# A two-layer recurrent decoder step on one core: small-tile work cut from VectorE, norm roots and first remainders moved off GpSimd, the planner's costs re-read from the trace

## The chip, the cores and the metric

One core of a Trainium2 chip runs the whole program. The metric is the device time of one execution in microseconds (us); the kernel before takes 1069.55 us, the median of three runs (1068.46 to 1069.59). About 0.2% of it, 2.1 us, is what a measurement of this kernel can tell from no change.

## What is computed

One inference step of a decoder with two layers, on 1024 prompt tokens and 8 x 4 sample tokens (1056 columns in all, model width 1024). Layer 0 is an RG-LRU block, layer 1 an HGRN2 block:

```
xn = rmsnorm(x) * g_norm                        # mean of squares over 1024 features, rsqrt, gain
u  = xn @ w_in;  xb, gate = u[:1536], u[1536:]  # layer 0: 1024 -> 3072
xc = causal_conv(xb, conv_w, conv_b)            # 4 taps
r, ig = sigmoid(xc @ w_r + b_r), sigmoid(xc @ w_i + b_i)   # 16 blocks of 96
log_a = -8 * softplus(-lam) * r;  a = exp(log_a)
h_t = a_t * h_(t-1) + sqrt(1 - a_t^2) * (ig * xc)_t        # a scan over time
x  = x + (h * silu(gate)) @ w_out
...                                             # layer 1: HGRN2, 1024 -> 4096, matrix states, 1024 -> 1024
y  = rmsnorm(x) * final_gain
```

The conv states, the hidden states and the matrix states are outputs too. Everything is float32. A product is made of three passes on TensorE: each operand is parted into a rounded "high" part and the "remainder" (value minus high), and high x high, high x remainder and remainder x high are added up in PSUM. So each weight tile and each activation tile costs a cast on ScalarE (high) and a subtraction on VectorE or GpSimd (remainder) before TensorE can use it.

## The kernel before

**Tiling.** Features lie on the 128 partitions, tokens on the free axis, in three chunks of 352 columns (`c` = 0, 1, 2). A weight is a block of 128 x 1024, loaded as two raw tiles of 128 x 512. `weights()` loads it, casts the high part on ScalarE (L388) and subtracts the remainder on the engine it is told (L333, in `subtract`).

**The start of layer 0** (`begin`, from L862). Six weight blocks (three of the gate, three of the conv branch, `items`) and the three chunks of x are loaded. For chunk 0 the high and remainder parts are made of x times the gain without waiting for the norm, which is applied to the products later (L490, L537). In parallel `squares` (L432 on) adds up the squares of the eight feature tiles of each chunk: the square on ScalarE (L440) or, for the pairs that the list `MU` names, on GpSimd (L438), the running sum on VectorE (L443). `norm` (L445) then makes the factor: a TensorE product with ones adds over the partitions (L286), two VectorE operations scale and add the epsilon (L455), GpSimd raises to the power -0.5 (L457), VectorE spreads the factors over two diagonals (L458, L461), and TensorE broadcasts them (L463). `scaled_parts` (L465) multiplies x by gain and factor on VectorE (L468), casts the high part on ScalarE (L469) and subtracts the remainder (L333) on VectorE, or on GpSimd for every fourth feature tile. `VI` names the weight blocks whose remainders VectorE makes: 0, 1, 2 and 4; those of 3 and 5 are GpSimd's.

Then come the 18 products of the six blocks with the three chunks, the convolution (L506 to L515), the gates of the recurrence (`lru`, L549: Tanh at L573 and L579, Exp at L586, Tanh at L588, Sqrt at L596, the scan at L613), and so on through layer 0. `norm` is called three times here and three times more near the end of layer 0 (`out_last`, L658), where layer 1's input is normed.

**Small tiles.** `smalls` (L748) works out per-feature constants from the parameters on tiles of 128 x 12: half the two gate biases (`hbr`, `hbi`), a rearranged copy of them for the 32-partition rows (`hbd`), and 8 * softplus in a form with one Exp and a polynomial of eight steps, as `cn` and `cp`. It issues 34 VectorE operations (recorded at L750) and one Exp on ScalarE (L761). Each `norm` adds a VectorE memset of its factor tile (L450), six in all. All operations of `smalls` write one key, `sm`, for which the Tanh of L573 and L579 wait, as do L586 and L588. `smalls1` (L782, recorded at L783) and `masks` (L804, recorded at L808) make constants of layer 1 in the same way; `masks` uses two of the five `k` buffers, which the norms and the recurrence use too.

**What sets the order.** No queue order is written by hand. Each operation is handed to a planner (`Flow.add`, L68) with its engine, a cost in us, what it reads and writes and a priority. `plan` simulates the engines on the host with these costs; `run` plans forward, then backward for due times, eight times over, and keeps the best; `search` tries 3000 variations of the first 60 us. The instructions are then issued in that order, a fixed queue for each engine. The costs: `HOP` is what a result takes to reach another engine; between two operations of the same engine `lag` is nothing. A VectorE operation costs 0.075 or 0.13 us and 0.00104 us for each column, a GpSimd operation 0.13 and 0.0022. Operations that are flagged `both` and GpSimd operations delay one another in the plan as if they shared a port. Small-tile operations (`seq`, L744) are planned at 0.1 us, without that flag. Layer 0 and layer 1 are planned one after the other by the same class.

Of the kernel before, what the change touches and what calls it, by code (L numbers as in the profile page):

```python
# [51 lines left out]
class Flow:  # L52

    HOP = {"PE": 0.22, "DVE": 0.14, "ACT": 0.14, "POOL": 0.14, "SP": 0.2}
    ENGINES = ("PE", "DVE", "ACT", "POOL", "SP")
    TURNS = 8
    ends = []
# [13 lines left out]
    def add(self, eng, us, emit, r=(), w=(), prio=5, kb=0, main=False, both=False):  # L73


        i = len(self.ops)
        deps = set()
        for k in r:
            if k in self.writer:
                deps.add(self.writer[k])  # L80
        for k in w:
            if k in self.writer:
                deps.add(self.writer[k])
            deps.update(self.readers.get(k, ()))
        if main:
            if self.main is not None:
                deps.add(self.main)
            self.main = i
        for k in w:
            self.writer[k] = i  # L90
            self.readers[k] = []
        for k in r:
            self.readers.setdefault(k, []).append(i)
        deps.discard(i)
        self.ops.append((eng, us, emit, deps, prio, kb, self.side if eng == "PE" and not main else 0.0, both))

    def lag(self, i, j):

        a, b = self.ops[i], self.ops[j]
        if a[0] == b[0] and not a[5]:  # L100
            return 0.0
        return self.HOP[a[0]] + b[6] + (2.15 + a[5] / 250.0 if a[5] else 0.0)

    def plan(self, key, stop=None):

        n = len(self.ops)
        left = [len(o[3]) for o in self.ops]
        ready = [0.0] * n
        wait = {e: [] for e in self.ENGINES}
        free = dict(self.busy)  # L110
        dma = locked = taken = 0.0
        for i in range(n):
            if not left[i]:
                wait[self.ops[i][0]].append(i)
        starts, ends, took, order = [0.0] * n, [0.0] * n, [0.0] * n, []
        for _ in range(n):
            t0, e = min((max(free[e], min(ready[i] for i in q)), e) for e, q in wait.items() if q)
            q = wait[e]
            i = min((j for j in q if ready[j] <= t0), key=lambda j: (key[j], j))
            q.remove(i)  # L120
            order.append(i)
            _, us, _, _, _, kb, _, both = self.ops[i]
# [95 lines left out]
def tile_trunk(ctx: ExitStack, tc: tile.TileContext, xT, prm, hc, w0, wg, wo0, w1, wo1, s_in,  # L218
# [22 lines left out]
    def pv(name):  # L241
        return P[:, PRM[name][0]:PRM[name][1]]
# [62 lines left out]
    with ExitStack() as l0:  # L305
# [20 lines left out]
            fl.add("DVE", own + 0.00104 * n, emit, r, w, prio, both=both)  # L326

        def pool(n, emit, r, w, prio=5):
            fl.add("POOL", 0.13 + 0.0022 * n, emit, r, w, prio)

        def subtract(e, n, b, x, a, r, w, prio):

# [15 lines left out]
            cycle([(wts.tile([128, 512], dt, tag=tag, bufs=n, name="w" + tag), (tag, i)) for i in range(n)])  # L348
            for tag, n, dt in (("raw", NRAW, F32), ("hi", NW, F32R), ("lo", NW, F32R)))
        nrs = cycle([(fixed(f"nr{i}", [128, 4]), ("nr", i)) for i in range(2)])  # L350
        xbs = ring("xb", 3, 384)
        ks = [(KR[:, chunk(i)], ("k", i)) for i in range(KB)]
        ts, xrs = cycle(ks[:3]), cycle(ks[3:])
# [88 lines left out]
                e = eng or G  # L442
                (pool if e is G else dve)(CH, lambda: e.tensor_tensor(a[:, :CH], a[:, :CH], sq, op=ALU.add), (sk, ak), (ak,), 2)  # L443

        def norm(acc, own=None):  # L445

            a, ak = acc
            r, rk = next(nrs)
            dg, dk = own or next(xbs)
            dve(4, lambda: V.memset(r, 1.0), (), (rk,), 0)  # L450
            f = CH // 128
            ps, pk = next(hg)
            fl.add("PE", 0.7, lambda: norm_sum([ps[:, i:i + 1] for i in range(4)], a, CH, True, True), (ak,), (pk,), 0)
            for q, src in ((slice(0, f), ps[:, :f]), (slice(f, f + 1), ps[:CH % 128, f:f + 1])):
                dve(4, lambda q=q, src=src: V.tensor_scalar(r[:src.shape[0], q], src, 1.0 / D, EPS, op0=ALU.mult, op1=ALU.add),  # L455
                    (pk,), (rk,), 0)
            fl.add("POOL", 0.9, lambda: G.tensor_tensor(r[:, :3], r[:, :3], mhalf[:, :3], op=ALU.pow), (rk,), (rk,), 0)  # L457
# [89 lines left out]
        def lru(g):  # L547
# [11 lines left out]
            for c in range(NCH):  # L559
# [5 lines left out]
                for i, hb in ((0, hbr), (1, hbi)):  # L565
                    for j in range(3):
                        m = 3 * g + j
                        ps, pk = next(hg)
                        (a, ak), (b, bk) = xpart(j, 0, c), xpart(j, 1, c)
                        u = 3 * i + j  # L570
                        fl.add("PE", 0.48, lambda ps=ps, a=a, b=b, u=u: mm3(ps[:, :CH], (gh[:, u, :], gl[:, u, :]), a, b, True, True),
                               (ak, bk, ("gh", u // 4 * 4), ("gl", u // 4 * 4)), (pk,), 0)
                        act(CH, lambda ps=ps, R=R, i=i, j=j, hb=hb, m=m: S.activation(R[:, i, j], ps[:, :CH], AF.Tanh, bias=hb[:, m:m + 1],  # L573
                                                                           scale=0.5), (pk, ("sm",)), (("R", s, i, j),), 2, 0.1)
                    ps, pk = next(hg)

                    fl.add("PE", 0.62, lambda ps=ps, i=i, c=c: T.matmul(ps[:96, :CH], gs[:, i, :], ST[:96, chunk(c)], start=True, stop=True),  # L577
                           (("gs",), *(("ST", j, c) for j in range(3))), (pk,), 0)
                    act(CH, lambda ps=ps, i=i: S.activation(td[:, i], ps[:96, :CH], AF.Tanh, bias=hbd[:96, 4 * i + g:4 * i + g + 1],  # L579
                                                            scale=0.5), (pk, ("sm",)), (("td", i),), 2, 0.1)  # L580
# [162 lines left out]
        def seq(keys, prio, *emits):  # L743

            for eng, emit in emits:
                fl.add(eng, 0.1, emit, (("P",),), keys, prio)

        def smalls():  # L748
            def v(f, *a, **k):
# [2 lines left out]
            def ttv(o, a, b, op):  # L752
                v(V.tensor_tensor, o, a, b, op=op)

            nonlocal hbr, hbi, hbd, cn, cp
            hbr, hbi, nl, t1, e, z, z2, po = (small(12) for _ in range(8))
            v(V.tensor_scalar, hbr, pv("br"), 0.5, None, op0=ALU.mult)
            v(V.tensor_scalar, hbi, pv("bi"), 0.5, None, op0=ALU.mult)
            v(V.tensor_scalar, nl, pv("lam"), -1.0, None, op0=ALU.mult)
            ttv(t1, pv("lam"), nl, ALU.min)  # L760
            seq((("sm",),), 0.5, ("ACT", lambda: S.activation(e, t1, AF.Exp)))  # L761
            v(V.tensor_scalar, t1, e, 2.0, None, op0=ALU.add)
            v(V.reciprocal, z, t1)
            ttv(z, z, e, ALU.mult)
            ttv(z2, z, z, ALU.mult)
            v(V.tensor_scalar, po, z2, 1.0 / 17, 1.0 / 15, op0=ALU.mult, op1=ALU.add)
            for d in (13, 11, 9, 7, 5, 3, 1):
                ttv(po, po, z2, ALU.mult)
                v(V.tensor_scalar, po, po, 1.0 / d, None, op0=ALU.add)
            ttv(po, po, z, ALU.mult)  # L770
            v(V.tensor_scalar, nl, nl, 0.0, None, op0=ALU.max)
            cp, cn = small(12), small(12)
            v(V.scalar_tensor_tensor, cp, po, 2.0, nl, op0=ALU.mult, op1=ALU.add)
            v(V.tensor_scalar, cn, cp, -4.0, None, op0=ALU.mult)
            v(V.tensor_scalar, cp, cp, 2.0, None, op0=ALU.mult)
            hbd = small(8)
            for i, hb in ((0, hbr), (1, hbi)):
                for j in range(3):
                    w = slice(32 * j, 32 * j + 32)
                    v(V.tensor_copy, hbd[w, 4 * i:4 * i + 4], hb[w].rearrange("p (g j) -> p g j", j=3)[:, :, j])  # L780
# [73 lines left out]
        g0s = [g0[:, k:k + 1] for k in range(KD)]  # L854
        bcs = free[11]
        accs = next(xbs), free[9], free[10]
        VI, XG, MU = (0, 1, 2, 4), (), [(0, k) for k in range(1, 8, 2)]
        rest = [(o[:, a:a + 512], ("a", i, a)) for i, o in enumerate(a_rows) for a in (0, 512)]
        rest += [(ST[:, :512], *(("ST", j, c) for j in range(3) for c in range(2)))]
        raw1 = [(), rest[:1], rest[1:3], rest[3:5], (), ()]  # L860
# [1 line left out]
        def begin(c, first, last):  # L862
# [20 lines left out]
                act(CH, lambda bc=bc: S.copy(bcs[0], bc), (bk,), (bcs[1],), 0)  # L883
            else:
                for k, (x, xk) in enumerate(raw[c]):
                    scaled_parts(c, k, x, xk, bc, bk, g0s[k], ("g0",), G if k % 4 == 3 else V)

        def products(c):
            for i in (2, 0, 1, 3, 4, 5) if c else range(6):
# [935 lines left out]
```

## Time and profile before

| | us |
|---|---|
| median of three runs | 1069.55 (1068.46 to 1069.59) |
| the profiled execution, its own time | 1070.2 |
| its span, first to last instruction | 1068.4 |
| busy: TensorE | 1042.6 (98%) |
| busy: VectorE | 809.9 (76%) |
| busy: ScalarE | 576.0 (54%) |
| busy: GpSimd | 498.9 (47%) |

How to read it: PE is TensorE, DVE VectorE, ACT ScalarE, POOL GpSimd, SP the engine that issues most DMAs. `L333` is line 333 of the kernel. A group or a row of the timeline shows start, duration, engine, line and tiles (`out<-in`). The chain of work that ended last is followed back from the last instruction: each of its pieces shows when it began, how long it held the chain, and the engine and line. "issue" is time for which the profile shows no wait. A table by stage shows for each stretch of the span its length, then the busy time of each engine with the number of its instructions, the granted TensorE clock (1.00 is full), the share of the DMA engines and GB/s.

### The profile page before, as it was taken

To read this page: it belongs to the slowest core of one execution; us is meant where nothing else is said; L and a number is where in the kernel's file an instruction comes from. 1 tells how busy PE (TensorE), PEld (TensorE's weight loads), DVE (VectorE), ACT (ScalarE), POOL (GpSimd) and SP (SyncE) were. 2 spreads that over 40 slices of the span, in tenths; PEclk is the share of its full clock that TensorE was granted. 3 is DMA by queue.
4 is the path that set the end of the run, shared out by engine and by line. 5 is a ranking of instruction groups with operands and counts; after the bars stand their busy time and mean duration, and the time that the engine had idled before them with its cause. 6 is when DMAs were issued, how large, how long until landed. Compare 5 with 4: busy or idle time off the path is not lost.

```text
span 1068.4 us, 26448 instructions
## 1 busy us (share of the span) xinstructions
PE 1042.6 (98%) x10244; PEld 1010.2 (95%) x10244; DVE 809.9 (76%) x1620; ACT 576.0 (54%) x1311; POOL 498.9 (47%) x587
## 2 busy tenths in 40 slices
PE   9898999999999999999999999999999999999997
PEld 8788999999999999999989999999999999999986
DVE  8998767589698789544487989797969796985536
ACT  5476645966856686434354463636454554552324
POOL 2425233445344355744524555555555555642544
PEclk9999999999999999999999999999999999999998
DMA  8201112212581388553374233332324242576204
GB/s 293 67 14 56 33 48 61 67 44 66 180 271 52 95 247 263 153 170 129 99 228 138 73 123 106 106 118 85 135 74 140 83 140 83 168 232 204 85 1 163
DMA packets 92013, 130.72 MB, mean 122 GB/s; under 512 B 11632, under 2 KB 70000, under 8 KB 91888
## 3 DMA queue, kind: packets, MB, share of 16 engines
q1 hardware_dynamic: 89584, 126.28, 37.1%
q10 hardware_dynamic: 2304, 2.77, 0.7%
q8 instruction: 80, 1.31, 0.5%
q14 instruction: 45, 0.37, 0.1%
HBM read 85.93 MB, written 38.20 MB: 116 GB/s over the span
## 4 chain that ended last, share of the span: by engine, by line
PE 86%; DVE 9%; issue 2%; DMA 1%; POOL 1%; ACT 0%; SPq 0%; POOLq 0%; DVEq 0%; ACTq 0%
PE mm L249 24%; PE mm L251 24%; PE mm L250 24%; PE hg L1066 2%; PE hg L1274 1%; PE hg L577 1%; PE hg L1276 1%; PE hg L250 1%; PE hg L251 1%; PE hg L249 1%; DVE xl L333 1%; DVE sg L468 1%; DVE R L443 1%; DVE k L509 1%; DVE smalls L750 1%
## 5 line engine op out<-in xcount | busy, mean ns | idle before, releaser
L249 PE MATMUL mm<-xh,whi 128*128 128x352 f32 (+1 forms) x1127 | 352.8, 313 | 0.0
L251 PE MATMUL mm<-xh,wlo 128*128 128x352 f32 (+1 forms) x1127 | 348.8, 310 | 0.0
L250 PE MATMUL mm<-xl,whi 128*128 128x352 f32 (+1 forms) x1127 | 348.4, 309 | 0.0
L333 POOL TENSOR_TENSOR wlo<-wraw,whi 128x256 fp32r<-128x256 f32 (+3 forms) x188 | 199.3, 1075 | 248.6 <-ACT whi L388 135.4
L250 PEld LDWEIGHTS mm<-xl,whi 128*128 128x128 f32 x1127 | 213.3, 189 | 1.5
L249 PEld LDWEIGHTS mm<-xh,whi 128*128 128x128 f32 x1127 | 212.9, 189 | 1.7
L251 PEld LDWEIGHTS mm<-xh,wlo 128*128 128x128 f32 x1127 | 213.0, 189 | 0.0
L509 DVE SCALAR_TENSOR_TENSOR k<-xb,prm_sb,k 128x352 f32<-128x352 f32 (+2 forms) x144 | 87.0, 615 | 23.1 <-ACT k L506 20.0
L249 PE MATMUL mm<-t,whi 128*128 128x264 f32 (+1 forms) x330 | 96.6, 293 | 1.4 <-DVE attns L1073 1.4
L250 PE MATMUL mm<-t,whi 128*128 128x264 f32 (+1 forms) x330 | 94.6, 287 | 0.0
L251 PE MATMUL mm<-t,wlo 128*128 128x264 f32 (+1 forms) x330 | 94.4, 286 | 0.0
L1504 DVE TENSOR_TENSOR k<-mm,k 128x264 f32<-128x264 f32 x154 | 64.4, 425 | 21.6 <-PE mm L251 20.2
L333 POOL TENSOR_TENSOR wlo<-R,whi 128x256 fp32r<-128x256 f32 x70 | 59.7, 873 | 29.7 <-ACT whi L1431 26.2
L592 POOL TENSOR_TENSOR k<-X 128x352 f32<-128x352 f32 x36 | 44.2, 1234 | 47.2 <-DVE R L593 32.8
L249 PEld LDWEIGHTS mm<-t,whi 128*128 128x128 f32 x330 | 62.1, 188 | 2.2 <-ACT krep L1006 1.6
L251 PEld LDWEIGHTS mm<-t,wlo 128*128 128x128 f32 x330 | 62.2, 189 | 0.0
L250 PEld LDWEIGHTS mm<-t,whi 128*128 128x128 f32 x330 | 62.2, 188 | 0.0
L1431 ACT CAST whi<-wraw 128x512 fp32r<-128x512 f32 x56 | 34.6, 617 | 45.8 <-PE mm L251 15.4
L388 ACT CAST whi<-wraw 128x512 fp32r<-128x512 f32 (+2 forms) x79 | 43.9, 572 | 24.9 <-PE mm L250 20.2
L249 PE MATMUL mm<-yh,whi 128*128 128x352 f32 x153 | 51.4, 336 | 0.0
L251 PE MATMUL mm<-yh,wlo 128*128 128x352 f32 x153 | 49.4, 323 | 0.0
L250 PE MATMUL mm<-yl,whi 128*128 128x352 f32 x153 | 49.4, 323 | 0.0
(460 smaller groups left out, 2520.0 us busy)
## 6 DMA issues: line engine op xcount, KB each, us to landing
wraw<-in_w_dram SPq DMA_DIRECT2D x88, 256.0 KB, 2.8
wraw<-in_wo_dram SPq DMA_DIRECT2D x34, 192.0 KB, 2.5
R<-in_w_dram SPq DMA_DIRECT2D x17, 256.0 KB, 2.7
si<-in_s_in_dram SPq DMA_DIRECT2D x8, 512.0 KB, 4.8
vt<-sg SPq DMA_DIRECT2D x8, 512.0 KB, 3.2
kt<-kt SPq DMA_DIRECT2D x8, 512.0 KB, 2.7
sg<-vt SPq DMA_DIRECT2D x32, 128.0 KB, 2.9
kt<-kt SPq DMA_DIRECT2D x32, 128.0 KB, 3.5
```

The costliest lines, as they stand in the source:

```text
L249: T.matmul(out, wh, xh, start=first, stop=False)
L250: T.matmul(out, wh, xl, start=False, stop=False)
L251: T.matmul(out, wl, xh, start=False, stop=last)
L333: emit = lambda: e.tensor_tensor(b, x, a.bitcast(F32), op=ALU.subtract)
L388: act(m, lambda hi=hi, raw=raw, m=m: S.copy(hi[:, :m], raw[:, :m]), rk, (hk,), prio)
L443: (pool if e is G else dve)(CH, lambda: e.tensor_tensor(a[:, :CH], a[:, :CH], sq, op=ALU.add), (sk, ak), (ak,), 2)
L468: dve(CH, lambda: V.scalar_tensor_tensor(x, x, g, bc, op0=ALU.mult, op1=ALU.mult), (xk, bk, gk), (xk,), prio)
L509: dve(u, lambda src=src, dst=dst, sh=sh, k=k: V.scalar_tensor_tensor(dst, sh(src, k), pc("cw", 12 * k + m), dst, op0=ALU.mult, op1=ALU.add ...
L592: pool(CH, lambda x=x, a=a, b=b: G.tensor_tensor(x, a.bitcast(F32), b.bitcast(F32), op=ALU.add), (ak, bk), (xk,), 3)
L1066: T.matmul(ps[32 * j:32 * j + 32, n * w:n * w + w], B[:, o:o + 32], q(slice(o, o + 32)), start=True, stop=True, tile_position=(0, 32 * j))
L1431: act(512, lambda: S.copy(hi, raw), (rk,), (hk,), 2)
L1504: dve(QT, lambda: V.tensor_tensor(o[0], z[0], u[0], op=ALU.add), (z[1], u[1]), (o[1],), 0)
```

## The change

It has four parts. (1) `smalls`: biases are halved and rearranged on ScalarE (one multiplication for both, three copies), under a key of their own, `smb`, for which alone L573 and L579 wait; the polynomial's steps are one fused operation each; `cn` and `cp` are made on ScalarE. (2) `norm`: the factor tile is set to one once, at the start; ScalarE takes Sqrt of sum / 1024 + epsilon, straight from PSUM, once for each 128 columns (three times), and VectorE takes one reciprocal. (3) `VI` takes in all six blocks, `MU` is empty, and the remainders of chunks 1 and 2 in `begin` (L886) are all VectorE's; those of chunk 0 (L898) and of `out_last` (L714) stay as they were, every fourth on GpSimd. (4) The planner: a result costs its own engine 0.1 us on VectorE and ScalarE (`SAME`), a GpSimd operation 0.15 instead of 0.13, a small-tile operation 0.09 instead of 0.1, and those of VectorE carry the flag `both`. The order is planned anew with these costs, for both layers.

```diff
+    SAME = {"DVE": 0.1, "ACT": 0.1}
...
         if a[0] == b[0] and not a[5]:
-            return 0.0
+            return self.SAME.get(a[0], 0.0) if i in b[8] else 0.0
...
-            fl.add("POOL", 0.13 + 0.0022 * n, emit, r, w, prio)
+            fl.add("POOL", 0.15 + 0.0022 * n, emit, r, w, prio)
...
         nrs = cycle([(fixed(f"nr{i}", [128, 4]), ("nr", i)) for i in range(2)])
+        for r, _ in islice(nrs, 2):
+            V.memset(r, 1.0)
...
-            dve(4, lambda: V.memset(r, 1.0), (), (rk,), 0)
-            f = CH // 128
-            ps, pk = next(hg)
-            fl.add("PE", 0.7, lambda: norm_sum([ps[:, i:i + 1] for i in range(4)], a, CH, True, True), (ak,), (pk,), 0)
-            for q, src in ((slice(0, f), ps[:, :f]), (slice(f, f + 1), ps[:CH % 128, f:f + 1])):
-                dve(4, lambda q=q, src=src: V.tensor_scalar(r[:src.shape[0], q], src, 1.0 / D, EPS, op0=ALU.mult, op1=ALU.add),
-                    (pk,), (rk,), 0)
-            fl.add("POOL", 0.9, lambda: G.tensor_tensor(r[:, :3], r[:, :3], mhalf[:, :3], op=ALU.pow), (rk,), (rk,), 0)
+            if sums is None:
+                ps, pk = next(hg)
+                sums, sumk = [ps[:, i:i + 1] for i in range(4)], [pk]
+                fl.add("PE", 0.7, lambda: norm_sum(sums, a, CH, True, True), (ak,), sumk, 0)
+            for i, (s, (_, u)) in enumerate(zip(sums, spans(CH))):
+                act(4, lambda i=i, s=s, u=u: S.activation(r[:u, i:i + 1], s[:u], AF.Sqrt, bias=epsc[:u], scale=1.0 / D), sumk, (rk,), 0,
+                    0.1 if i else 0.8)
+            dve(4, lambda: V.reciprocal(r[:, :3], r[:, :3]), (rk,), (rk,), 0, True)
...
-                                                                           scale=0.5), (pk, ("sm",)), (("R", s, i, j),), 2, 0.1)
+                                                                           scale=0.5), (pk, ("smb",)), (("R", s, i, j),), 2, 0.1)
...
-                fl.add(eng, 0.1, emit, (("P",),), keys, prio)
+                fl.add(eng, 0.09, emit, (("P",),), keys, prio, both=eng == "DVE")
...
-            hbr, hbi, nl, t1, e, z, z2, po = (small(12) for _ in range(8))
-            v(V.tensor_scalar, hbr, pv("br"), 0.5, None, op0=ALU.mult)
-            v(V.tensor_scalar, hbi, pv("bi"), 0.5, None, op0=ALU.mult)
-            v(V.tensor_scalar, nl, pv("lam"), -1.0, None, op0=ALU.mult)
-            ttv(t1, pv("lam"), nl, ALU.min)
-            seq((("sm",),), 0.5, ("ACT", lambda: S.activation(e, t1, AF.Exp)))
+            hb, nl, t1, e, z, z2, po, cp, cn = small(24), *(small(12) for _ in range(8))
+            hbd, hbr, hbi = small(8), hb[:, :12], hb[:, 12:]
+            other(lambda: S.mul(hb, P[:, PRM["br"][0]:PRM["bi"][1]], 0.5), "smb")
+            for j in range(3):
+                w = slice(32 * j, 32 * j + 32)
+                other(lambda w=w, j=j: S.copy(hbd[w].rearrange("p (i g) -> p i g", i=2), hb[w].rearrange("p (i g j) -> p i g j", i=2, j=3)[:, :, :, j]), "smb")
+            v(V.scalar_tensor_tensor, t1, pv("lam"), -1.0, pv("lam"), op0=ALU.mult, op1=ALU.min)
+            other(lambda: S.activation(e, t1, AF.Exp))
+            v(V.tensor_scalar, nl, pv("lam"), -1.0, 0.0, op0=ALU.mult, op1=ALU.max)
...
-            for d in (13, 11, 9, 7, 5, 3, 1):
-                ttv(po, po, z2, ALU.mult)
-                v(V.tensor_scalar, po, po, 1.0 / d, None, op0=ALU.add)
-            ttv(po, po, z, ALU.mult)
-            v(V.tensor_scalar, nl, nl, 0.0, None, op0=ALU.max)
...
+            ttv(po, po, z2, ALU.mult)
+            for d in (13, 11, 9, 7, 5, 3):
+                v(V.scalar_tensor_tensor, po, po, 1.0 / d, z2, op0=ALU.add, op1=ALU.mult)
+            v(V.scalar_tensor_tensor, po, po, 1.0, z, op0=ALU.add, op1=ALU.mult)
+            v(V.scalar_tensor_tensor, nl, po, 2.0, nl, op0=ALU.mult, op1=ALU.add)
+            other(lambda: S.mul(cn, nl, -4.0))
+            other(lambda: S.mul(cp, nl, 2.0))
...
-        VI, XG, MU = (0, 1, 2, 4), (), [(0, k) for k in range(1, 8, 2)]
+        VI, XG, MU = range(6), (), ()
...
-                    scaled_parts(c, k, x, xk, bc, bk, g0s[k], ("g0",), G if k % 4 == 3 else V)
+                    scaled_parts(c, k, x, xk, bc, bk, g0s[k], ("g0",), V)
```

More of the change, by code (lines that the diff above doesn't have):

```diff
@@ L77, in add @@
         deps = set()
-        for k in r:
+        for k in (*r, *w):
             if k in self.writer:
                 deps.add(self.writer[k])
+        written = frozenset(deps)
         for k in w:
-            if k in self.writer:
-                deps.add(self.writer[k])
             deps.update(self.readers.get(k, ()))
@@ L94, in add @@
         deps.discard(i)
-        self.ops.append((eng, us, emit, deps, prio, kb, self.side if eng == "PE" and not main else 0.0, both))
+        self.ops.append((eng, us, emit, deps, prio, kb, self.side if eng == "PE" and not main else 0.0, both, written))
     def lag(self, i, j):
@@ L121, in plan @@
             order.append(i)
-            _, us, _, _, _, kb, _, both = self.ops[i]
+            _, us, _, _, _, kb, _, both, _ = self.ops[i]
             if both:
@@ L443, in squares, with norm @@
                 (pool if e is G else dve)(CH, lambda: e.tensor_tensor(a[:, :CH], a[:, :CH], sq, op=ALU.add), (sk, ak), (ak,), 2)
-        def norm(acc, own=None):
+        def norm(acc, own=None, sums=None, sumk=()):
             a, ak = acc
@@ L579, in lru @@
                     act(CH, lambda ps=ps, i=i: S.activation(td[:, i], ps[:96, :CH], AF.Tanh, bias=hbd[:96, 4 * i + g:4 * i + g + 1],
-                                                            scale=0.5), (pk, ("sm",)), (("td", i),), 2, 0.1)
+                                                            scale=0.5), (pk, ("smb",)), (("td", i),), 2, 0.1)
                     for j in range(3):
@@ L753, in ttv, with other @@
                 v(V.tensor_tensor, o, a, b, op=op)
+            def other(emit, key="sm"):
+                seq(((key,),), 0.5, ("ACT", emit))
             nonlocal hbr, hbi, hbd, cn, cp
-            hbr, hbi, nl, t1, e, z, z2, po = (small(12) for _ in range(8))
-            v(V.tensor_scalar, hbr, pv("br"), 0.5, None, op0=ALU.mult)
-            v(V.tensor_scalar, hbi, pv("bi"), 0.5, None, op0=ALU.mult)
-            v(V.tensor_scalar, nl, pv("lam"), -1.0, None, op0=ALU.mult)
-            ttv(t1, pv("lam"), nl, ALU.min)
-            seq((("sm",),), 0.5, ("ACT", lambda: S.activation(e, t1, AF.Exp)))
+            hb, nl, t1, e, z, z2, po, cp, cn = small(24), *(small(12) for _ in range(8))
[7 more added lines that the diff above has]
+            v(V.tensor_scalar, nl, pv("lam"), -1.0, 0.0, op0=ALU.mult, op1=ALU.max)
             v(V.tensor_scalar, t1, e, 2.0, None, op0=ALU.add)
@@ L766, in smalls @@
             v(V.tensor_scalar, po, z2, 1.0 / 17, 1.0 / 15, op0=ALU.mult, op1=ALU.add)
-            for d in (13, 11, 9, 7, 5, 3, 1):
-                ttv(po, po, z2, ALU.mult)
-                v(V.tensor_scalar, po, po, 1.0 / d, None, op0=ALU.add)
-            ttv(po, po, z, ALU.mult)
-            v(V.tensor_scalar, nl, nl, 0.0, None, op0=ALU.max)
[L772 to L780, printed above, removed]
+            ttv(po, po, z2, ALU.mult)
[5 more added lines that the diff above has]
+            other(lambda: S.mul(cp, nl, 2.0))
         def smalls1():
```

## The prediction

> **What bounds the kernel now.** I read the page first, then a table by stage, then the waits of TensorE, then the chain in order of time. Two lines of the page:
>
> ```profile
> PE 1042.6 (98%) x10244; PEld 1010.2 (95%) x10244; DVE 809.9 (76%) x1620; ACT 576.0 (54%) x1311; POOL 498.9 (47%) x587
> PE 86%; DVE 9%; issue 2%; DMA 1%; POOL 1%; ACT 0%; SPq 0%; POOLq 0%; DVEq 0%; ACTq 0%
> ```
>
> TensorE is the bound over all, but 9% of the chain, some 96 us, is VectorE's. The stages (columns: stretch, its length, then busy PE, PEld, DVE, ACT, POOL with their counts, the granted clock, DMA share, GB/s) show where:
>
> ```profile
> 0.00:22.00 22.00, 20.75 (x141) 20.28 (x141) 17.42 (x57) 12.35 (x26) 5.66 (x13) 1.00 0.91 309
> 22.00:40.00 18.00, 12.26 (x73) 10.49 (x73) 17.19 (x46) 9.55 (x21) 7.81 (x7) 0.98 0.39 126
> 40.00:60.00 20.00, 17.93 (x95) 16.08 (x95) 19.93 (x46) 11.54 (x26) 6.77 (x13) 0.93 0.11 31
> 60.00:88.00 28.00, 25.19 (x153) 24.41 (x152) 26.43 (x70) 19.08 (x40) 8.24 (x11) 0.98 0.05 13
> 88.00:150.00 62.00, 62.00 (x373) 61.03 (x373) 46.96 (x83) 42.25 (x79) 23.91 (x31) 0.98 0.17 49
> 150.00:500.00 350.00, 350.00 (x2150) 345.21 (x2149) 254.93 (x416) 216.78 (x427) 165.50 (x177) 1.00 0.45 138
> 500.00:1000.00 500.00, 492.68 (x6879) 476.53 (x6878) 393.25 (x837) 239.24 (x626) 248.61 (x302) 1.00 0.39 127
> ```
>
> From 88 to 500 us TensorE never rests, so nothing that the change does there can make it shorter. From 22 to 88 us it is busy 12.26 + 17.93 + 25.19 = 55.4 of 66 us, while VectorE is busy 17.19 + 19.93 + 26.43 = 63.6 of them. TensorE's waits between 0 and 88 us (who waited, for whom, us, times, longest) nearly all name VectorE:
>
> ```profile
> PE hg L250 <- DVE X L515: 2.8, 1, 2.8
> PE hg L286 <- DVE R L443: 2.7, 2, 1.9
> PE hg L463 <- DVE k L461: 1.9, 2, 1.4
> PE hg L286 <- DVE xb L443: 1.3, 1, 1.3
> ```
>
> And the chain in order of time is VectorE's queue almost without a break until this point, where it passes to TensorE for good:
>
> ```profile
> 87.11 0.53 DVE X L515
> ...
> 87.69 0.66 PE hg L250
> ```
>
> So the first 88 us last as long as VectorE's queue, and a microsecond taken from that queue there is one taken from the whole, until TensorE or the transfers become the limit. All that the change edits by hand, but three of the six norms, lies in this stretch.
>
> **Part 1: what GpSimd's going away returns to VectorE.** These pieces of the chain (start, us held, what) lasted far longer than their like:
>
> ```profile
> 6.19 0.67 DVE smalls L750
> ...
> 7.35 0.18 DVE smalls L750
> ...
> 14.70 0.60 DVE wlo L333
> 15.30 0.69 DVE smalls L750
> 16.01 1.21 DVE smalls L750
> ...
> 20.75 0.44 DVE R L443
> ...
> 27.61 1.25 DVE smalls L750
> ...
> 31.78 1.66 DVE R L443
> ...
> 35.87 1.62 DVE R L443
> ...
> 56.72 1.01 DVE sg L468
> 57.73 0.49 DVE R L468
> ...
> 60.20 0.44 DVE xl L333
> ```
>
> GpSimd's timeline has an operation under each; two of the seven:
>
> ```profile
> 31.74 1.30 POOL L333 TENSOR_TENSOR yl<-wraw,yh 128x512 fp32r<-128x512 f32 x1 [0.83 <-ACT yh L388]
> ...
> 56.42 0.93 POOL L333 TENSOR_TENSOR xl<-R,xh 128x352 fp32r<-128x352 f32 x1 [2.86 <-ACT xh L469]
> ```
>
> The sum at 31.78 begins 0.04 us after GpSimd's 1.30 us and holds the chain 1.66 us instead of 0.44: VectorE stood still until GpSimd was done. The Trainium skill says so too (SBUF — State Buffer, section "Who interferes with whom"): the two engines share a port pair, held for a whole instruction, and the later one waits. By that rule the wait goes when the GpSimd operation goes, and the trace agrees with its 1.22 us.
>
> The excess over the like (0.18 for a small tile, 0.44 for L443, 0.49 for L468) is 0.49 + 0.51 + 1.03 + 1.07 + 1.22 + 1.18 + 0.52 = 6.0 us. All seven fall under work that the change takes off GpSimd: the squares of `MU`, the remainders of blocks 3 and 5 (`yl`), a remainder of chunk 1 or 2. Two such pieces stay, under chunk 0's remainders, which GpSimd keeps:
>
> ```profile
> 64.55 1.19 DVE sg L468
> ...
> 69.89 0.87 DVE k L808
> ```
>
> The price: VectorE gets four remainders of 512 columns, at 0.60 (14.70 above), and four of 352, at 0.44 (60.20 above): 2.4 + 1.8 = 4.2 us. The four squares on ScalarE lie beside it: ScalarE is busy 12.35 of the first 22 us. Part 1 alone: 6.0 - 4.2 = 1.8 us saved.
>
> **Part 2: the small tiles.** By the code `smalls` falls from 34 VectorE operations to 16. One that waits for the one before it holds the chain 0.18 us (7.35 above), so 18 x 0.18 = 3.2 us go. The seven small operations that ScalarE gets instead are off the chain. Their users, L573 and L586, come with the recurrence, well behind.
>
> **Part 3: the norms.** Each loses two VectorE operations and the power on GpSimd, and gains a reciprocal (median in the middle):
>
> ```profile
> L455 DVE TENSOR_SCALAR nr<-hg x12: 142/150/160, 26.9 to 506.8; 128x2 f32<-128x2 f32 x6, 96x1 f32<-96x1 f32 x6
> ...
> L457 POOL TENSOR_TENSOR nr<-nr,mhalf x6: 859/1002/1207, 29.7 to 507.0; 128x3 f32<-128x3 f32 x6
> ...
> L750 DVE RECIPROCAL smalls<-smalls x1: 228/228/228, 6.9 to 6.9; 128x12 f32<-128x12 f32 x1
> ```
>
> On VectorE: 2 x 0.15 - 0.23 = 0.07 for each of three, 0.2 us; the removed memset I take at nothing. The power's 1.0 us is replaced by three roots on ScalarE, and these need the table of Sqrt. Before, no Sqrt stands ahead of 76 us. What a change of table costs is seen at L596 and at the return to Tanh:
>
> ```profile
> L596 ACT ACT_TABLE_LOAD  x12: 1283/1283/1283, 76.1 to 403.3; - x12
> ...
> 87.73 1.28 ACT L541 ACT_TABLE_LOAD   x1
> 89.03 0.46 ACT L541 ACTIVATE sg<-mm 128x352 f32<-128x352 f32 x1
> ```
>
> One load takes 1.283 us, and the next instruction begins 1.30 us after the load did. The plan charges 0.88 us for the first root and nothing for the way back. Three visits cost at most 3 x 2 x 1.30 = 7.8 us of ScalarE, at least one pair (2.6) if the three norms and the Tanhs of the gates do not alternate. ScalarE idles (18 - 9.55) + (20 - 11.54) = 16.9 us between 22 and 60 us, so the loads fit. What falls on VectorE's queue, which stands still when its next operation waits for ScalarE, is bounded by 0 and 7.8; I take 0.6, near the low end, since in those stages ScalarE is idle nearly half the time and its chain share is 0%.
>
> The Trainium skill weighs against this part (ScalarE: Activation LUTs, section "What ACT_TABLE_LOAD costs"): it puts a switch at about 2.66 us, the load and then a drain of 1.38 us. By that, six switches would take 16 us of ScalarE, and the sum would come out slower; the trace's 1.30 us to the next instruction does not show the drain.
>
> **Part 4: the order.** Dependent small operations now cost 0.19 in the plan, so it may put other work between them. `masks` shows what that is worth:
>
> ```profile
> 23.54 0.08 DVE smalls L750
> ...
> 73.84 0.19 DVE mask L808
> ```
>
> One that waits for its forerunner holds the chain 0.19 us, one that does not 0.08. `masks` has 33 operations by the code, all in this stretch, and `smalls` 16 then: between 0 and 49 x 0.11 = 5.4 us. I take 1.0, near the low end, as the queue has little independent work left in that stage. A new order can also be worse; for layer 1 I take nothing, bounded by a fifth of the 500 - 492.68 = 7.3 us that TensorE rests between 500 and 1000 us, 1.5 either way. The last three norms lie here:
>
> ```profile
> L461 DVE TENSOR_SCALAR xb<-ident,nr x3: 264/1207/1296, 459.6 to 508.3; 128x96 f32<-128x96 f32 x3
> ```
>
> Between 150 and 500 us TensorE's own work hides them, and ScalarE, busy 216.78 of 350 us, has room for their loads. The last one lies behind 500 us; if its cover failed, two loads, 2.6 us, would show.
>
> **The sum.** 1.8 + 3.2 + 0.2 + 1.0 - 0.6 = 5.6 us off the profiled execution's 1070.2: 1064.6. The median of the runs is 0.65 below that execution: 1063.9. What is late next: the part of TensorE's rest that remains, and the two GpSimd remainders of chunk 0.
>
> **The rivals.**
> *More than the sum (1059.5).* The order fills the gaps (3 of the 5.4 us more) and TensorE's clock, 0.93 between 40 and 60 us, no longer dips (0.07 x 20 = 1.4): 1063.9 - 4.4 = 1059.5. For it: VectorE is full, so each gap counts. Against it: TensorE's rest up to 88 us is 10.6 us, some of it the waits of the norms, which stay. If all that rest and the 1.4 went, it would be 1070.2 - 12 - 0.65 = 1057.5, the far end.
> *No change (1068.6).* Another feeder takes over in the first 40 us: the DMA engines are 91% busy up to 22 us, and the raw tiles come when they come. VectorE then waits for data where it waited for GpSimd. Only what lies behind 40 us is gained, 0.5 (56.72) and the filled gaps, 1.0, less 0.6: 0.9 us, 1070.2 - 0.9 - 0.65 = 1068.6. Against it: DMA falls to 39% after 22 us, and half the waits lie behind 22 us.
> *Slower (1072).* The loads land on VectorE's queue. Place: the three roots between 22 and 60 us, ahead of casts (L469) and Tanhs (L538) that VectorE waits for. Price: 1.30 us for each load that is not covered. It decides when more than 5.6 + 0.6 = 6.2 us of loads, five of the six, are uncovered. With all six, 7.8 us instead of the 0.6 in the sum, and the 1.0 of filled gaps lost to the disturbed order: 1063.9 + 7.2 + 1.0 = 1072.1. For it: the return load is not in the plan at all. Against it: 16.9 us of idle time.
> *A switch holds ScalarE twice as long as its load (1074).* Then six switches of 2 x 1.30 us are 15.6 us, and meet 16.9 us of idle time that lies in pieces; with two thirds uncovered, 10.4 us on VectorE's queue, the time is 1063.9 + 10.4 = 1074.3. This is the rule of the page named in part 3. I give it 0.02, since the row at 89.03 speaks against it.
>
> **How the numbers follow.** The forecast 0.52, more 0.26, no change 0.11, slower 0.09, the rule 0.02. About 0.2%, 2.1 us, can be told from no change, so faster is below 1067.4: 0.78; within 0.11; slower 0.11. The range reaches from 1057.5 to 1070, which leaves out the slower cases and a part of no change.
>
> **What would show it.** Right: GpSimd's busy time before 88 us, 5.66 + 7.81 + 6.77 + 8.24 = 28.5 us, falls by 12 us (four `yl` of 1.3, four `xl` of 0.93, three powers of 1.0) and by the four squares; the pieces of over 1 us under L443 and L750 are gone; the chain passes to TensorE near 82 us instead of 87.7; from there the stages are as long as before. Wrong: ScalarE's loads between 22 and 60 us with VectorE or TensorE idle behind them; VectorE as full as before but with TensorE no earlier; or a rest of TensorE between 88 and 500 us, where there was none.

## The result, and the profile after

The changed kernel takes 1057.65 us, the median of four runs (1057.09 to 1057.92), beside 1069.57 for the kernel before: a ratio of 0.9888, 95% interval 0.9871 to 0.9905. That is 11.9 us, more than twice the 5.6 that were forecast, and just inside the lower end of the range (1057.5). Its profiled execution took 1057.09 us, with a span of 1055.3. The shares of the chain of work that ended last, first line of that part of the page:

```profile
PE 92%; DVE 3%; ACT 2%; DMA 1%; issue 1%; POOL 0%; SPq 0%; ACTq 0%; POOLq 0%; DVEq 0%
```

VectorE's share fell from 9% to 3%, and ScalarE, which had none, has 2%. The table by stage of the changed kernel (columns as before the prediction):

```profile
0.00:22.00 22.00, 20.96 (x141) 20.97 (x142) 15.36 (x42) 18.41 (x40) 0.86 (x9) 1.00 0.89 292
22.00:40.00 18.00, 15.11 (x97) 13.83 (x96) 13.40 (x34) 16.64 (x33) 2.42 (x4) 1.00 0.47 151
40.00:60.00 20.00, 17.96 (x106) 16.29 (x106) 19.80 (x42) 12.24 (x26) 3.99 (x6) 1.00 0.09 27
60.00:88.00 28.00, 28.00 (x169) 27.06 (x169) 25.29 (x86) 21.60 (x45) 4.19 (x11) 1.00 0.07 17
...
500.00:1000.00 500.00, 494.95 (x6911) 478.43 (x6911) 396.83 (x852) 246.11 (x653) 276.40 (x310) 1.00 0.40 130
```

Up to 88 us TensorE is busy 82.0 us instead of 76.1, its clock no longer dips, GpSimd's work fell from 28.5 to 11.5 us. Between 500 and 1000 us TensorE rests 5.0 us instead of 7.3. And between 22 and 40 us the full engine is not VectorE (13.40 of 18) but ScalarE (16.64). The chain in order of time shows it (here L457 is a norm's Sqrt, L540 a Tanh of a gate):

```profile
23.13 1.28 ACT L457
...
30.93 1.28 ACT L540
32.21 0.01 issue
32.22 0.89 ACT k L540 x2
33.11 0.01 issue
33.11 1.28 ACT L457
...
36.22 1.28 ACT L540
...
45.13 1.28 ACT L457
...
50.07 0.43 PE mm L250
```

Five table loads of 1.28 us lie on the chain, before it passes to TensorE at 50 us instead of 87.7. The timeline of ScalarE has eight switches of table before 54 us; the first three:

```profile
19.54 1.28 ACT L457 ACT_TABLE_LOAD   x1
20.83 0.26 ACT L457 ACTIVATE nr<-hg,eps 128x1 f32<-128x1 f32 x1
21.10 1.28 ACT L796 ACT_TABLE_LOAD   x1
22.39 0.21 ACT L796 ACTIVATE smalls<-smalls 128x8 f32<-128x8 f32 x1
...
23.13 1.28 ACT L457 ACT_TABLE_LOAD   x1
24.42 0.26 ACT L457 ACTIVATE nr<-hg,eps 128x1 f32<-128x1 f32 x1
```

The planner put an Exp of `smalls1` (L796) between the first and the second root of one norm. For the plan that costs 0.09 us; on the chip it cost two loads.

**Where the 13.1 us of span came from.** A landmark that all kernels have is the last square ahead of layer 1's norms (last start in the row of that line). Up to it a kernel's time is layer 0's. What follows I call layer 1's, though it begins a little earlier; the source view of the kernel before, then of the changed one:

```profile
L440 ACT ACTIVATE k<-sg x18: 496/498/500, 437.7 to 503.0; 128x352 f32<-128x352 f32 x18
```

```profile
L442 ACT ACTIVATE k<-sg x18: 497/498/501, 429.9 to 494.3; 128x352 f32<-128x352 f32 x18
```

Layer 0 gave 503.0 - 494.3 = 8.7 us; layer 1 gave (1068.4 - 503.0) - (1055.3 - 494.3) = 4.4.

### The profile page after: what moved, and what is told of

It is laid out like the page before. It is cut to its first block, busy times and chain, and to the rows that moved or that the text cites. A ratio compares the mean times of both kernels' runs of the same rounds, so it can differ in the third digit from the quotient of the medians.

```text
span 1055.3 us, 26461 instructions
## 1 busy us (share of the span) xinstructions
PE 1037.3 (98%) x10244; PEld 1006.9 (95%) x10244; DVE 795.6 (75%) x1600; ACT 594.2 (56%) x1350; POOL 503.7 (48%) x569
## 4 chain that ended last, share of the span: by engine, by line
PE 92%; DVE 3%; ACT 2%; DMA 1%; issue 1%; POOL 0%; SPq 0%; ACTq 0%; POOLq 0%; DVEq 0%
PE mm L249 26%; PE mm L250 25%; PE mm L251 25%; PE hg L1068 2%; PE hg L579 1%; PE hg L1276 1%; PE hg L1278 1%; PE hg L249 1%; PE hg L251 1%; PE hg L250 1%; PE mm L1221 1%; PE hg L1221 1%; PE hg L1320 1%; DMA sg<-in_xT_dram 1%; ACT L457 0%
## 5 line engine op out<-in xcount | busy, mean ns | idle before, releaser
L333 POOL TENSOR_TENSOR wlo<-wraw,whi 128x256 fp32r<-128x256 f32 (+3 forms) x188 | 214.9, 1160 | 180.1 <-ACT whi L390 92.6
L511 DVE SCALAR_TENSOR_TENSOR k<-xb,prm_sb,k 128x352 f32<-128x352 f32 (+2 forms) x144 | 81.2, 588 | 24.7 <-ACT k L508 21.7
L333 POOL TENSOR_TENSOR wlo<-R,whi 128x256 fp32r<-128x256 f32 x70 | 57.4, 841 | 36.9 <-ACT whi L1433 36.7
```

Source lines behind the costliest of these rows:

```text
L333: emit = lambda: e.tensor_tensor(b, x, a.bitcast(F32), op=ALU.subtract)
L511: dve(u, lambda src=src, dst=dst, sh=sh, k=k: V.scalar_tensor_tensor(dst, sh(src, k), pc("cw", 12 * k + m), dst, op0=ALU.mult, op1=ALU.add ...
```

## The experiments

Eighteen kernels ran beside these two. Most have a part of the change alone, or the change without a part; three have another seed of the planner's search, two another lag, one has its masks moved. "Part" numbers are those of the section on the change. The two right columns split the span of the profiled execution at the landmark.

| kernel | us | ratio to before, 95% interval | landmark | rest |
|---|---|---|---|---|
| before | 1069.57 | | 503.0 | 565.4 |
| changed | 1057.65 | 0.9888 (0.9871 to 0.9905) | 494.3 | 561.0 |
| plan_only | 1054.73 | 0.9857 (0.9842 to 0.9873) | 491.1 | 562.1 |
| plan_other_seed | 1055.08 | 0.9859 (0.9842 to 0.9876) | 491.0 | 562.7 |
| before_other_seed | 1069.43 | 0.9998 (0.9988 to 1.0007) | 503.8 | 562.4 |
| lag_alone | 1060.50 | 0.9911 (0.9890 to 0.9931) | 494.8 | 563.7 |
| lag_vector_only | 1061.29 | 0.9929 (0.9908 to 0.9949) | 494.0 | 565.2 |
| lag_three_times | 1059.73 | 0.9906 (0.9890 to 0.9922) | 495.2 | 563.5 |
| lag_off_in_layer1 | 1063.07 | 0.9933 (0.9914 to 0.9951) | 495.3 | 567.3 |
| hand_only | 1065.09 | 0.9949 (0.9931 to 0.9967) | 496.4 | 567.2 |
| smalls_alone | 1063.48 | 0.9945 (0.9930 to 0.9959) | 494.2 | 567.2 |
| off_gpsimd_alone | 1063.20 | 0.9942 (0.9927 to 0.9957) | 493.8 | 566.9 |
| norm_alone | 1070.62 | 1.0004 (0.9995 to 1.0013) | 500.7 | 568.3 |
| hand_without_norm | 1063.40 | 0.9938 (0.9923 to 0.9953) | 492.5 | 567.6 |
| masks_late | 1066.47 | 0.9965 (0.9953 to 0.9977) | 496.7 | 567.4 |
| plan_and_norm | 1055.96 | 0.9866 (0.9848 to 0.9885) | 492.5 | 561.6 |
| all_but_norm | 1050.65 | 0.9819 (0.9801 to 0.9836) | 487.4 | 561.5 |
| squares_back | 1050.85 | 0.9823 (0.9809 to 0.9838) | 486.8 | 561.3 |
| squares_back_seed | 1050.89 | 0.9814 (0.9800 to 0.9829) | 487.7 | 560.9 |
| both_undone | 1050.74 | 0.9819 (0.9802 to 0.9835) | 487.7 | 560.8 |

The kernel before ran beside each group, at 1069.2 to 1070.9 us in the median; the ratio is the fairer comparison. A profiled execution can lie off its kernel's median (before_other_seed 1.4 us and hand_without_norm 1.5 below, lag_off_in_layer1 1.4 above), so a difference of 1 or 2 us in the two right columns is not clear of noise.

**plan_only: part 4 alone, on the kernel before.**

```diff
+    SAME = {"DVE": 0.1, "ACT": 0.1}
...
-            fl.add("POOL", 0.13 + 0.0022 * n, emit, r, w, prio)
+            fl.add("POOL", 0.15 + 0.0022 * n, emit, r, w, prio)
...
-                fl.add(eng, 0.1, emit, (("P",),), keys, prio)
+                fl.add(eng, 0.09, emit, (("P",),), keys, prio, both=eng == "DVE")
```

> Only the planner's costs are changed (same-engine lag, GpSimd 0.15, small tiles 0.09 and flagged); no instruction is added or removed, only the order. Theory A (two sources: VectorE's queue in the first 88 us, and layer 1's new order, which showed 3.9 us of the 13.1 us of span): layer 1's 4 us come here, and 1 to 3 at the start, 1062.5 to 1065. Rival B (the hand edits alone made the gain): 1069.5. Rival C (each new order moves the time by chance): anywhere between 1060 and 1075.

Measured 1054.73, below the range of every theory: not an instruction changed, only their order, and it is faster than the whole change. Theory A had put 1 to 3 us on layer 0; it was 11.9. Its table by stage:

```profile
0.00:22.00 22.00, 20.97 (x142) 20.83 (x143) 15.55 (x41) 13.35 (x28) 7.61 (x14) 1.00 0.87 286
22.00:40.00 18.00, 16.71 (x102) 15.06 (x101) 17.92 (x49) 10.81 (x23) 7.81 (x8) 1.00 0.57 183
40.00:60.00 20.00, 19.66 (x121) 18.94 (x122) 19.95 (x49) 10.53 (x23) 7.80 (x9) 1.00 0.02 5
60.00:88.00 28.00, 28.00 (x171) 27.30 (x170) 26.33 (x81) 16.05 (x37) 9.69 (x16) 1.00 0.17 50
```

VectorE is as full as before (79.8 of 88 us, before 81.0), and GpSimd has more to do than before, yet TensorE is busy 85.3 us. Which work VectorE does in that time, not how much, is what changed.

**hand_only: parts 1 to 3, the planner's old costs.**

```diff
-            return self.SAME.get(a[0], 0.0) if i in b[8] else 0.0
+            return 0.0
...
-            fl.add("POOL", 0.15 + 0.0022 * n, emit, r, w, prio)
+            fl.add("POOL", 0.13 + 0.0022 * n, emit, r, w, prio)
...
-                fl.add(eng, 0.09, emit, (("P",),), keys, prio, both=eng == "DVE")
+                fl.add(eng, 0.1, emit, (("P",),), keys, prio)
```

> All edits but the planner's costs, which are the old ones. Theory A: the start keeps some 6 to 8 us of its gain, layer 1 gives none, 1061.5 to 1064. Rival B: all of it, 1057.7. Rival C: no telling.

Measured 1065.09, a gain of 4.5, and 1.1 above theory A's range: layer 0 gave 6.6 us, as it had said, and layer 1 took 1.8 back. Rival B falls with these two: the edits by hand are the smaller source.

**lag_off_in_layer1: the changed kernel, layer 1 planned without the lag.**

```diff
         fl = Flow(side=0.4, busy={e: max(0.0, t - last["PE"]) for e, t in last.items()})
+        fl.SAME = {}
```

> The changed kernel, but layer 1 is planned without the same-engine lag; layer 0 is planned as in the changed kernel. Theory A: TensorE's rest between 540 and 1000 us comes back, 1060.5 to 1062. If layer 1's part does not hang on the lag (rival B, or the start of layer 1 set by how layer 0 ends): 1057.7.

Measured 1063.07, 1.1 us more than theory A's range, so some 5.4 us of the changed kernel hang on the lag in layer 1. The kernels planned without it have a rest of 565.4 to 568.3 us in eight of nine cases, those with it on both engines at its 0.1 us 560.8 to 563.7. The ninth is before_other_seed at 562.4 (its seed steers the search of layer 1's start too): the luck of an order may give there a part of what the lag gives. Two stretches show what moved, first without the lag, then the changed kernel:

```profile
520.00:530.00 10.00, 10.00 (x64) 10.00 (x63) 3.36 (x7) 2.32 (x5) 3.18 (x5) 1.00 0.51 150
550.00:560.00 10.00, 7.64 (x167) 7.23 (x166) 9.86 (x21) 4.53 (x10) 0.92 (x1) 1.00 0.30 96
```

```profile
520.00:530.00 10.00, 10.00 (x64) 10.00 (x63) 7.03 (x14) 3.52 (x10) 4.37 (x4) 1.00 0.79 241
550.00:560.00 10.00, 10.00 (x166) 9.63 (x162) 9.15 (x20) 5.03 (x14) 0.71 (x2) 1.00 0.17 49
```

With the lag in its costs the plan starts VectorE's work for layer 1 earlier (7.03 us of 10 instead of 3.36), and TensorE does not wait for it 25 us later. Without the lag it does, in two waits of 1.7 and 0.7 us; the longer:

```profile
PE hg L1069 <- DVE R L1051: 1.7, 1, 1.7
```

**masks_late: the kernel before, the masks moved behind the first recurrence.**

```diff
         smalls1()
-        masks()
...
         lru(0)
+        masks()
         split_y(0)
```

> The kernel before, but the 33 small operations of the masks are handed to the planner after the first recurrence instead of before it, so that they need not be done in the first 80 us. Theory A: they held the chain there for some 6 us, which the changed order moved off it; 1063 to 1065. Rival (they only filled gaps, and the excess over the forecast is TensorE's clock and the norms): 1068.5 to 1069.5.

Measured 1066.47, 3.1 us faster, between the two forecasts. Layer 0 gave 6.3, as theory A had it: the masks held the chain. Layer 1 gave 2.0 of it back, which theory A had not said. Moving the masks is not the only way to layer 0's gain: in smalls_alone and off_gpsimd_alone below they still hold the chain, from 72.7 and 73.7 us, and layer 0 is 8.8 and 9.2 us shorter.

**all_but_norm: parts 1, 3 and 4; the norms' root stays a power on GpSimd.** The edit is the removed lines of `norm` in the change, put back.

> The changed kernel with the norms as they were before (two VectorE operations and the power on GpSimd, no Sqrt on ScalarE). Theory D (the new costs of the planner made the gain, and the hand edits lose some 3 us on top of them, because the Sqrts bring seven table loads ahead of 60 us and fill ScalarE to 16.6 of 18 us between 22 and 40 us): the loss goes, 1052 to 1055. Rival E (what is lost lies in VectorE's eight more remainders, not in the norms): 1057 to 1058.

Measured 1050.65, 7 us faster than the changed kernel, more than theory D's "some 3".

**plan_and_norm: parts 2 and 4.**

> The kernel before with the planner's new costs and the norms' roots on ScalarE; small tiles and remainders as before. Theory D: it loses 2 to 4 us against the planner's costs alone (1054.7), so 1057 to 1059. Rival E: 1054 to 1055.5.

Measured 1055.96, between the two forecasts: the norms on ScalarE lose 1.2 us here, which a measurement cannot tell from nothing, and 7 in the changed kernel. Yet between 22 and 40 us ScalarE is fuller here (17.33 of 18 us) than in the changed kernel, and TensorE rests nearly as much:

```profile
22.00:40.00 18.00, 15.47 (x101) 14.97 (x99) 13.08 (x32) 17.33 (x36) 4.09 (x4) 1.00 0.43 138
```

There are eight switches of the table here too, five of them on the chain before 60 us, and Tanhs split a norm's roots. So neither the roots, nor the number of switches, nor a full ScalarE in that stretch is enough for the loss of 7 us.

**plan_other_seed.** As plan_only, with

```diff
-        rng = Random(1)
+        rng = Random(2)
```

> The planner's new costs alone, with another seed of its search over the first 60 us: the same costs, another order. Theory D (the costs do it): within 1.5 us of 1054.7. Rival C (chance of an order): 3 us or more away from it.

Measured 1055.08: the costs do it under two orders, so not one lucky one.

**lag_alone: of part 4 only `SAME`.**

> Of the planner's new costs only the same-engine lag of 0.1 us; GpSimd's cost and that of the small tiles, with their flag, as before. If the lag is what matters: layer 1's 4 to 6 us and some of layer 0's 12 us, 1055 to 1059. If the small tiles' flag (their wait for GpSimd, now in the plan) made layer 0's part: layer 1 alone, 1063.5 to 1066.

Measured 1060.50, between the two forecasts. The lag gives 9.3 us; the rest of part 4, GpSimd's 0.15 and the small tiles' cost and flag, 5.8 more on top of it. Layer 0 has 8.2 us already with the lag.

**off_gpsimd_alone: part 3 with the old costs; smalls_alone: part 1 with the old costs.**

> The kernel before with one part of the change: the squares, the remainders of blocks 3 and 5 and those of chunks 1 and 2 off GpSimd; the planner's old costs. The prediction's term for this part: 1.8 us, so 1067 to 1069. Rival (waiting behind GpSimd cost more than the seven pieces show): 1062 to 1065. Rival (ScalarE or VectorE full): slower than 1070.

> The kernel before with one part of the change: the small tiles of layer 0, 34 VectorE operations to 16; the planner's old costs. The prediction's term: 3.2 us, so 1065.5 to 1067.5. Rival (with the old costs they only move the gap): 1069 to 1070.

Measured 1063.20 and 1063.48, 6.0 and 5.7 us faster: both far more than their terms of 1.8 and 3.2.

**lag_vector_only and lag_three_times: part 4 with another lag.**

```diff
-    SAME = {"DVE": 0.1, "ACT": 0.1}
+    SAME = {"DVE": 0.1}
```

> The planner's new costs alone, with the same-engine lag on VectorE only, none on ScalarE. If VectorE's dependent operations are what the plan had wrong: within 1.5 us of the 1054.7 with both. If ScalarE's lag matters as much (roots, casts, Tanhs in pairs): 1057 to 1062.

```diff
-    SAME = {"DVE": 0.1, "ACT": 0.1}
+    SAME = {"DVE": 0.3, "ACT": 0.3}
```

> The planner's new costs alone, with a same-engine lag of 0.3 instead of 0.1 us on both engines, three times what the rows show. Theory F (the gain comes from a cost that fits the rows): part of it is lost, 1057 to 1064. Rival G (any lag that keeps dependent operations apart does it): 1053 to 1056.

Measured 1061.29 and 1059.73. Taking ScalarE's lag out costs 6.6 us, three times the lag 5.0. Of the lags tried, the one that the rows show is the best, as theory F had it; but three times too much still leaves 9.5 us of gain over the kernel before. The other costs of part 4 without any lag were not run.

**before_other_seed: the kernel before with `Random(2)`.**

> The kernel before, nothing changed but the seed of the planner's search over the first 60 us: the same costs and instructions, another order at the start. Theory C' (the order of the kernel before was an unlucky one, so that nearly any change at the start gives 6 to 9 us by the end of layer 0): 1061 to 1065. Theory A' (each part takes its own time out of VectorE's queue, and they overlap): 1068.5 to 1070.5.

Measured 1069.43, ratio 0.9998: no unlucky order that just any other mends, as far as one other seed can show. It had been a fair suspicion, since nearly every variant gained 6 us or more in layer 0.

**hand_without_norm: parts 1 and 3, old costs; norm_alone: part 2, old costs.**

> The kernel before with the small tiles and the work off GpSimd, the norms as before, the planner's old costs. Alone these parts gave 5.7 and 6.0 us. If they add: 1057 to 1059. If the start has only some 9 us to give by either: 1061 to 1063.5. Together with the norms' roots on ScalarE it was 1065.1, so the norms' price under the old costs is the difference.

> The kernel before with the norms' roots on ScalarE alone, the planner's old costs. The prediction's term: 0.2 gained, 0.6 lost, so 1069 to 1070.5. Theory D (table loads on the chain): 1071 to 1074. Theory C' (any new order helps): 1061 to 1066.

Measured 1063.40, as if the start had only some 9 us to give, and 1070.62, 0.1 above what the prediction's term gives. Parts 1 and 3 do not add: 8.8 and 9.2 us of layer 0 alone, 10.5 together. The norms cost 1065.09 - 1063.40 = 1.7 us on top of them, hardly clear of noise, and nothing alone.

**squares_back: the changed kernel with the four squares on GpSimd again.**

```diff
-        VI, XG, MU = range(6), (), ()
+        VI, XG, MU = range(6), (), [(0, k) for k in range(1, 8, 2)]
```

> The changed kernel with the four squares of chunk 0 back on GpSimd, and so 2 us off ScalarE in the first 20 us. Theory D' (the Sqrts' loads cost 7 us because ScalarE is full by then with the squares and the small tiles): 2 to 4 us faster than the changed kernel, 1053.5 to 1055.5. If it is the loads themselves, wherever ScalarE stands: 1057 to 1058.5.

Measured 1050.85, 7 us faster, more than D' had said. Its table by stage, and the switches of ScalarE's table in its timeline up to 46 us:

```profile
0.00:22.00 22.00, 20.97 (x148) 20.97 (x148) 16.79 (x35) 16.42 (x36) 4.66 (x13) 1.00 0.90 290
22.00:40.00 18.00, 17.39 (x113) 16.56 (x113) 17.17 (x46) 15.87 (x38) 3.14 (x6) 1.00 0.56 178
40.00:60.00 20.00, 20.00 (x124) 19.59 (x122) 19.92 (x53) 13.22 (x27) 1.43 (x4) 1.00 0.03 8
```

```profile
22.14 1.28 ACT L457 ACT_TABLE_LOAD   x1
...
28.73 1.28 ACT L795 ACT_TABLE_LOAD   x1
...
33.44 1.28 ACT L457 ACT_TABLE_LOAD   x1
...
45.14 1.28 ACT L543 ACT_TABLE_LOAD   x1 [1.57 <-PE mm L251]
```

Four switches instead of eight, with the same nine roots, and no norm's roots are split any more; VectorE works 17.17 of 18 us between 22 and 40 us instead of 13.40, and TensorE 17.39 instead of 15.11.

**both_undone: all_but_norm with the four squares on GpSimd. squares_back_seed: squares_back with `Random(2)`.**

> The changed kernel with the norms as before and the four squares of chunk 0 on GpSimd as before. Theory D' (ScalarE full at the start; relieving it once is enough): 1049.5 to 1052, as with either alone. If the two losses are separate and add: 1043 to 1046.

> The changed kernel with the four squares on GpSimd, and another seed of the planner's search. Theory D': 1049.5 to 1052.5, as with the first seed. If its 7 us were the luck of an order: 1054 to 1059.

Measured 1050.74 and 1050.89. Relieving ScalarE twice gives no more than once, and the gain holds under another order. The four kernels at 1050.7 to 1050.9 beat both the kernel before and the changed one; none of them is measurably the best.

## Why the prediction was wrong

Here "Part" numbers are the prediction's: 1 is the work taken off GpSimd, 2 the small tiles, 3 the norms, 4 the order (in the section on the change, and in the experiments above, these are 3, 1, 2 and 4).

**What bounds the kernel: right, and the stretch too.** From 88 us to the landmark TensorE was full before and is full after. Of layer 0's 8.7 us, 5.9 are rest that TensorE no longer has in the first 88 us (82.0 us busy instead of 76.1); in the other 2.8 the same matmuls took less time, 488.3 us instead of 491.1 up to the landmark. The chain left VectorE at 50 us, not near 82, because the order could put off work that I had taken as fixed: the masks ran from 69.8 us on the chain before, and from 75 us beside a full TensorE after. Moving them, with the new order that this brings, was worth 6.3 us of layer 0 in masks_late. (TensorE's rest of 10.6 us that the prediction gives for "up to 88 us" is that from 22 us on; from the start it is 11.9.)

**Part 4 is the step that failed.** The prediction priced the new costs by the gaps that they might fill, "I take 1.0, near the low end", and layer 1 at nothing, bounded by 1.5 either way. Alone they give 14.9 us: 11.9 in layer 0, 3.3 in layer 1 (spans). On top of the hand edits they give 1065.09 - 1057.65 = 7.4, and since those gave 4.5 where 4.6 was forecast, 7.4 instead of 1.0 is the whole of what the sum had wrong. The bound of 5.4 us was no bound. It counted gaps between small operations, but the costs decide which work VectorE does first, and so how long TensorE rests behind it; the price of that is TensorE's rest, up to the 12 us (rest and clock) that I had named only as the far end. In layer 1 I bounded by a share of TensorE's rest, chosen without a reason.

**Part 1 and part 2, 1.8 and 3.2 us, were too small, each alone.** Alone they gave 6.0 and 5.7 us. The wait behind GpSimd went as part 1 had it: of the sums of over 1 us in the changed kernel's first 88 us one is left (1.17 us at 39.10, beside GpSimd's 1.29 us from 38.59 on a gate weight). The instruction sums left out how much of TensorE's rest goes with a shorter VectorE queue: off_gpsimd_alone keeps TensorE busy 83.6 of the first 88 us, where it was 76.1. Together they give 6.6 us: with both TensorE is busy 83.1 of the 88 us, no more than with one (83.6 and 83.1). (ScalarE gets six new small operations, not seven: its Exp was there before.)

**Part 3's price was right alone and wrong in company.** norm_alone shows no difference, as the sum of 0.2 and -0.6 had it. But "the four squares on ScalarE lie beside it" failed: with squares, small tiles and roots ScalarE is busy 18.41 of 22 and 16.64 of 18 us, eight switches lie there where I counted at most six, and the changed kernel loses 7 us of what its other parts give. The rival named slower had the right place, loads on the chain between 22 and 60 us, and nearly the price; part 4's gain covered it. Either relief of ScalarE, the norms or the squares back on GpSimd, brings the 7 us back, each under a new order, so the loss needs both on ScalarE. It needs the planner's new costs too: hand_only has both there and loses 1.7. By what path stays open: plan_and_norm has as many switches and as full a ScalarE between 22 and 40 us, and loses 1.2. The Exp that splits a norm's roots is in the changed kernel's trace; that it matters is not shown. The changed kernel itself was not run under another seed, so a share of luck in its order is not excluded.

**The hand edits' sum, 1.8 + 3.2 + 0.2 - 0.6 = 4.6 us, met hand_only's 4.5 by luck:** parts 1 and 2 gave 6.6 together instead of 5.0, and the norms took 1.7 instead of 0.4. By the split, layer 0 gave 6.6 and layer 1, taken as nothing, lost 1.8.

**A switch that holds ScalarE twice as long as its load** did not show: at 21.10 the load is followed by its Exp at 22.39, 1.29 us later.

## What to carry to other kernels

Where a planner on the host writes the order, its cost table is part of the kernel: price a change of costs by the rest that the bounding engine has in the stretch, not by the gaps between the operations repriced, and run it alone first. When work is moved to an idle engine, add up all that the change moves there in that stretch, and look for switches of its function table that the plan does not know of. Parts that each relieve the same full queue do not add.

## What the runs showed of the hardware

The 13.1 us of span are 7.8 us less rest of TensorE (1068.4 - 1042.6 = 25.8 before, 1055.3 - 1037.3 = 18.0 after) and 5.3 us less busy time of the same 10244 matmuls. Busy time of the changed kernel, from its page:

```profile
PE 1037.3 (98%) x10244; PEld 1006.9 (95%) x10244; DVE 795.6 (75%) x1600; ACT 594.2 (56%) x1350; POOL 503.7 (48%) x569
```

The granted clock goes the same way: the kernel before has 0.93 to 0.98 in the stretches from 22 to 150 us, the changed kernel 1.00 in each, and the mean over the span rose from 0.991 to 0.997. A pair with one order in layer 0 shows what such a dip goes with: lag_off_in_layer1 was granted 0.91 from 22 to 60 us where the changed kernel had 1.00, its matmuls up to the landmark were busy 489.9 us instead of 488.3, and it reached the landmark 1.0 us later. The mean clock does not foretell a run's time, though: of the kernel before, one run at 0.989 took 1069.33 us and one at 0.994 took 1070.66. That TensorE's rest brings the lower clock about is not shown here.
